# Two f32 transformer blocks on one core: token halves in a fixed order where token-major layers end, three held pieces of weights, the FFN input in wide operations, an even rate for the modulation

## The chip, the cores and the metric

The kernel runs on one core of one Trainium2 chip. The metric is device time of one launch in microseconds (us). All arithmetic that counts is f32: a matmul operand is split into a rounded high part and a low remainder, and three matmuls (high·high, high·low, low·high) stand for one product.

## The reference

Two blocks over 256 tokens and width 2048. The part that the change touches is the end of the first block, its FFN, and every layer whose result is wanted with tokens on partitions:

```python
mod = (c @ w_mod[l] + b_mod[l]).reshape(B, N_MOD, D)          # six segments of 2048
shift_f, scale_f, gate_f = mod[:, 3, None], mod[:, 4, None], mod[:, 5, None]
...
mix_out = merged @ w_out[l]
x = x + gate_m * rms_norm(mix_out, g_post_mix[l])
h2 = rms_norm(x, g_pre_ffn[l]) * (1 + scale_f) + shift_f
f = (jax.nn.silu(h2 @ w_ffn_gate[l]) * (h2 @ w_ffn_up[l])) @ w_ffn_down[l]
x = x + gate_f * rms_norm(f, g_post_ffn[l])
...
x = x + (y * jax.nn.silu(gate)) @ w_out_a[i]                   # second block, first layer
x = x + (merged * jax.nn.silu(gate)) @ w_out_b[i]              # second block, last layer
return rmsnorm(x, norm_f)
```

## The kernel before

Weights come from HBM in loads of 1 MB (`raw`, three buffers, issued on SP's queue). `stream_` cuts each load into pieces of 1024 columns: ACT casts a piece to its high part `wh` (L134), DVE subtracts to get `wl` (L135). There are three buffers of each (`SPL`), so a fourth piece can be cast only when TensorE is done with the first.

Most layers (`lin`) give features on partitions. Token-major layers (`linT`: w_out, the FFN's gate and up weights w_fgu, w_ffn_down as w_fd, w_outa, w_outb) give 128 tokens on partitions: there are two token halves, h = 0 and 1, each with its own PSUM banks, and every piece is used for both (12 matmuls of 512 columns in a piece, six in each half). A piece is used at once for both halves, except that the last load's two pieces are held and used for half 0 first, then for half 1.

The order of instructions on each engine is not the written one. A list scheduler with its own model of times takes whatever it holds ready, the written order being the priority; so it may interleave the halves. `issue_after(i)` pins what a block writes behind instruction i on its engine. `high_priority` lets weight loads and splits go ahead of older work; from the first block's second part on (`first`), all pieces have it.

`post` is the end of w_out and of w_fd: for each half, square sums from PSUM (ACT, L252), times a gate row (DVE, L930), the row statistic (DVE, then a power on GpSimd, L260), the update of x in four slices (DVE, L922), its square sums (ACT). Behind w_out the FFN input follows: the statistic again, x scaled into `mix` (ACT, L725), TensorE transposes 128x128 blocks into PSUM (L729, L739), and `modulated` makes each chunk of 128 features: high part on ACT (L714), scaled value on DVE (L715), low part on DVE (L716). Chunks 0 to 7 are made half by half, chunks 8 to 15 for both halves. Then the FFN starts; `XF` (Fh, Fl) is its input. Behind w_fd x is transposed (`turned`, L241) and split to `A`, the input of w_ina.

The matrix-vector product c @ w_mod is made by the side, one tile of 128x1024 (0.5 MB) at a time (`mod_tile`: a load on SP's queue and one DVE operation, L460). 96 tiles belong to the first block; `side` asks for `rate` of them at every 1 MB weight load. `mod_flush` sums 16 tiles over partitions on TensorE (L442). The last 32 of the 96 are the shift of the FFN input. In w_fd, `H(k)` splits two chunks of the hidden state at a time (L339 on ACT, L340 on DVE) into one of four places of `hx`, and keeps the last pair for the calls that follow.

Of the kernel before, what the change touches and what calls it, by code (L numbers as in the profile page):

```python
# [9 lines left out]
F32 = mybir.dt.float32  # L10
F32R = mybir.dt.float32r
AF = mybir.ActivationFunctionType
ALU = mybir.AluOpType
# [3 lines left out]
P = 128  # L17
T = 256
D = 2048
KC = D // P  # L20
# [6 lines left out]
SPL = 3  # L27
# [1 line left out]
SCALE = 128.0 ** -0.5  # L29


ORDER = "m2 m3 m4 G2 g9 g10 k0 k1 v7 v8 S r3 Q A r4 p0 p1 p2 G3 p3"

PACE = (3, 1)

# [54 lines left out]
class Kern:  # L90
# [19 lines left out]
    def stream(self, src, n, per):  # L110
        return list(self.pieces(src, n, per))

    def pieces(self, src, n, per):

        got = self.stream_(src, n, per)
        for a in range(0, n, per):
            if self.first:
                with self.tc.high_priority():
                    hl = next(got)
                if self.side and a + per >= n:  # L120
                    self.side()
            else:
                hl = next(got)
            yield hl

    def stream_(self, src, n, per):

        nc = self.nc
        raw = self.wp.tile([P, 2048], F32, name="raw", tag="raw", bufs=RAW)
        self.load = nc.sync.dma_start(raw[:, :n], src)  # L130
        for a in range(0, n, per):
            wh = self.wp.tile([P, 1024], F32R, name="wh", tag="wh", bufs=SPL)
            wl = self.wp.tile([P, 1024], F32R, name="wl", tag="wl", bufs=SPL)
# [63 lines left out]
    def linT(self, W, sb, X, nk, kper, ncols, which="a", lead=0, mid=None):  # L197
# [5 lines left out]
        ng = nk // kper  # L203
        mm = self.nc.tensor.matmul

        def run(h, k, wh, wl, o):
            xh, xl = X(k)
            t = slice(h * P, (h + 1) * P)
            for q in range(nq):
                w = slice(o + q * 512, o + q * 512 + 512)  # L210
                mm(banks[h][q], xh[:, t], wh[:, w], start=k == 0, stop=False, skip_group_check=True)  # L211
                mm(banks[h][q], xh[:, t], wl[:, w], start=False, stop=False, skip_group_check=True)  # L212
                mm(banks[h][q], xl[:, t], wh[:, w], start=False, stop=k == nk - 1, skip_group_check=True)  # L213
# [11 lines left out]
        for kg in range(ng):  # L225
            for i, (wh, wl) in enumerate(self.pieces(W[sb, kg], kper * ncols, 1024)):
                held.append((kg * kper + i * pk, wh, wl))
# [243 lines left out]
    def block1(self, c1):  # L471
        nc, tc, A = self.nc, self.tc, self.A
# [216 lines left out]
            self.row_in(0, grow[i], i * 1024, 1024)  # L689
        gs = self.cp.tile([P, 16], F32, name="gsf")  # L690

        def between(s, last):
            if s == 0:
                with tc.issue_after(last.ins):
                    self.load_x(nc.scalar)
            if s == 2:
                self.side = None
                for t in todo:
                    self.mod_tile(new, *t)
                self.mod_flush()  # L700
                nc.vector.scalar_tensor_tensor(gs, self.mods[:, 64:80], 1.0, self.vcol("g_pre_ffn", 0, 16), ALU.add, ALU.mult)

        mix = [p1e.tile([P, 8 * T], F32, name="mix%d" % h, tag="E1", bufs=2) for h in range(2)]
        ss, update = self.post(A["w_out"], XO, KC, mix, lambda c: grow[c // 2][:, c % 2 * 512:c % 2 * 512 + 512],
                               between=between)
# [12 lines left out]
        xn = []  # L718
        for h in range(2):
            update(h)  # L720
            self.rsum(r, ss, h)
            for c in range(4):

                m = mix[h][:, c * 512:(c + 1) * 512]
                nc.scalar.activation(m, self.xt[h][:, c * 512:(c + 1) * 512], AF.Copy, scale=r[:, h:h + 1])  # L725
                if c < 2:
                    bank = self.acc("b")
                    for b in range(4):
                        nc.tensor.transpose(bank[:, b * P:(b + 1) * P], m[:, b * P:(b + 1) * P], self.ident)  # L729
                    tmp = self.sp.tile([P, 512], F32, name="tm", tag="th", bufs=2)  # L730
                    for b in range(4):
                        s = slice(b * P, (b + 1) * P)
                        modulated(4 * c + b, slice(h * P, (h + 1) * P), bank[:, s], tmp[:, s])
        for k in range(8, KC, 2):
            bank = self.acc("b")
            tmp = self.sp.tile([P, 512], F32, name="tm", tag="th", bufs=2)
            for b in range(2):
                for h in range(2):
                    nc.tensor.transpose(bank[:, b * T + h * P:b * T + (h + 1) * P], mix[h][:, (k + b) * P:(k + b + 1) * P],  # L739
                                        self.ident)  # L740
                s = slice(b * T, (b + 1) * T)
                modulated(k + b, slice(0, T), bank[:, s], tmp[:, s])

# [156 lines left out]
    def post(self, W, X, nk, mix, G, wide=False, between=None):  # L900

        nc = self.nc
        nq = 2 if wide else 1
        last = 4 // nq - 1
        sm, sx = self.sums("sm4"), self.sums("sx4")
        r = self.rtile()
        for s in range(last + 1):
            banks = self.linT(W, s, X, nk, 2 if wide else 4, nq * 512, which="ba"[s % 2] if wide else "a")
            if s == last:
                break  # L910
            for h in range(2):
# [12 lines left out]
        return sx, update  # L924
# [175 lines left out]
    def ffn(self):  # L1100
        nc, tc, A = self.nc, self.tc, self.A
        with ExitStack() as c:
# [28 lines left out]

            for s in range(FFN // 256):

                banks = self.linT(A["w_fgu"], s, self.XF, KC, 4, 512, lead=0 if s else 3, mid=mid)
                t = self.sp.tile([P, 512], F32, name="ht", tag="sw", bufs=3)
                g = self.sp.tile([P, 512], F32, name="gt", tag="gt", bufs=2)
                for h in range(2):
                    a, bank = slice(h * T, (h + 1) * T), banks[h][0]
                    self.silu2(g[:, a], bank[:, :T], T)
                    nc.vector.tensor_mul(t[:, a], g[:, a], bank[:, T:])  # L1140
                due.append((s, t))
                for _ in range(3):
                    if todo and s:
                        with tc.issue_after(ready.ins):
                            self.mod_tile(new, *todo.pop(0))
                if s == 14:
                    self.mod_flush()
# [161 lines left out]
    def add_out(self, W, X, row=None, each=None, final=None):  # L1309
# [163 lines left out]
```

## Time and profile before

| | us |
|---|---|
| median of 3 runs (2441.3 to 2444.39) | 2444.15 |
| the profiled execution | 2438.1 |
| its span, first to last instruction | 2436.1 |
| TensorE busy in it | 2378.1 (98%) |
| VectorE (DVE) busy | 1678.5 (69%) |
| ScalarE (ACT) busy | 1246.7 (51%) |
| GpSimd (POOL) busy | 19.3 (1%) |
| mean granted TensorE clock | 0.991 |

The profiled execution is 6.05 us below the median of the runs. Times in the profile are from the start of the span. PE is TensorE, PEld its weight loads, SP the queue that issues DMAs. A matmul's duration includes its way through the array; matmuls overlap, so the distance from start to start counts, not the duration.

### The profile page before, as it was taken

Reading aid. Unit: us, or ns where it says so; the run is one execution under the profiler, and the core shown is the slowest. Engines: PE = TensorE matmul, PEld = TensorE weight load, DVE = VectorE, ACT = ScalarE, POOL = GpSimd, SP = SyncE. Lnnn points to the kernel's source line nnn. Section 1 sums busy time; section 2 is a strip of 40 time slices with the busy share of each in tenths; the row PEclk is TensorE's granted clock in tenths of the full one; section 3 lists DMA queues with packets and bytes.
Section 4 is the critical chain, followed back from the end, with each engine's and each line's share of the span. In section 5 each row is a group of like instructions: output and inputs, shape, how many; then the busy total and the mean of one; then the engine's idle time right before and its main releaser. Section 6 shows DMA issues by size and latency. Waiting matters only on the chain.

```text
span 2436.1 us, 37172 instructions
## 1 busy us (share of the span) xinstructions
PE 2378.1 (98%) x15142; PEld 2153.9 (88%) x15142; DVE 1678.5 (69%) x2213; ACT 1246.7 (51%) x1716; POOL 19.3 (1%) x30
## 2 busy tenths in 40 slices
PE   7999999999989999999999989999999999999997
PEld 6899989999868888888888879998898899999986
DVE  8997898888777575555556566756664477777764
ACT  5877674534464444444445454445644455554543
POOL 0000000000000000000000000000000000000000
PEclk9999999999999999999999999999999999999999
DMA  9997557999948585555555545555655544454453
GB/s 365 349 365 259 182 177 272 329 350 333 350 161 321 191 291 193 190 189 187 194 197 200 190 149 191 191 189 186 228 193 190 190 163 167 158 189 169 161 190 138
DMA packets 104043, 540.61 MB, mean 222 GB/s; under 512 B 9888, under 2 KB 18240, under 8 KB 53184
## 3 DMA queue, kind: packets, MB, share of 16 engines
q1 hardware_dynamic: 100896, 526.19, 60.8%
q10 hardware_dynamic: 2160, 8.88, 1.0%
q0 software_dynamic: 816, 3.16, 0.4%
q8 instruction: 118, 1.93, 0.3%
q14 instruction: 53, 0.43, 0.1%
HBM read 533.99 MB, written 4.21 MB: 221 GB/s over the span
## 4 chain that ended last, share of the span: by engine, by line
PE 94%; DVE 2%; ACT 1%; DMA 1%; issue 1%; POOL 0%; SPq 0%; DVEq 0%; POOLq 0%
PE acca L145 15%; PE acca L144 15%; PE acca L146 15%; PE acca L212 11%; PE acca L211 11%; PE acca L213 11%; PE acca L193 2%; PE acca L194 2%; PE acca L192 2%; PE accb L212 2%; PE accb L213 2%; PE accb L211 2%; DMA hid<-in_w_mod_dram 1%; DVE wl L135 1%; PE accb L1343 1%
## 5 line engine op out<-in xcount | busy, mean ns | idle before, releaser
L135 DVE TENSOR_TENSOR wl<-raw,wh 128x1024 fp32r<-128x1024 f32 x802 | 977.9, 1221 | 570.9 <-ACT wh L134 568.3
L134 ACT CAST wh<-raw 128x1024 fp32r<-128x1024 f32 x802 | 841.7, 1051 | 864.0 <-PE acca L213 377.9
L145 PE MATMUL acca<-Ql,wh 128*128 128x256 f32 x1024 | 290.5, 284 | 0.0
L144 PE MATMUL acca<-Qh,wh 128*128 128x256 f32 x1024 | 289.8, 284 | 0.0
L146 PE MATMUL acca<-Qh,wl 128*128 128x256 f32 x1024 | 285.5, 281 | 0.0
L212 PE MATMUL acca<-wl,Fh 128*128 128x512 f32 x704 | 276.8, 393 | 1.0 <-DVE wl L135 0.9
L213 PE MATMUL acca<-wh,Fl 128*128 128x512 f32 x704 | 275.7, 393 | 0.3 <-DVE Fl L716 0.3
L211 PE MATMUL acca<-wh,Fh 128*128 128x512 f32 x704 | 252.3, 396 | 1.7 <-ACT Fh L714 1.7
L144 PE MATMUL acca<-xh,wh 128*128 128x256 f32 x832 | 232.8, 284 | 4.5 <-ACT xh L808 3.4
L145 PE MATMUL acca<-xl,wh 128*128 128x256 f32 x832 | 233.7, 284 | 0.0
L146 PE MATMUL acca<-xh,wl 128*128 128x256 f32 x832 | 227.0, 283 | 0.0
L144 PEld LDWEIGHTS acca<-Qh,wh 128*128 128x128 f32 x1024 | 192.9, 188 | 0.5
L145 PEld LDWEIGHTS acca<-Ql,wh 128*128 128x128 f32 x1024 | 192.6, 188 | 0.8
L146 PEld LDWEIGHTS acca<-Qh,wl 128*128 128x128 f32 x1024 | 192.1, 189 | 0.4
L144 PEld LDWEIGHTS acca<-xh,wh 128*128 128x128 f32 x832 | 158.1, 190 | 7.3 <-ACT xh L808 3.6
L145 PEld LDWEIGHTS acca<-xl,wh 128*128 128x128 f32 x832 | 157.4, 189 | 1.6 <-issue 0.7
L212 PEld LDWEIGHTS acca<-wl,Fh 128*128 128x128 f32 x704 | 132.7, 189 | 29.1 <-DVE wl L135 2.2
L211 PEld LDWEIGHTS acca<-wh,Fh 128*128 128x128 f32 x704 | 131.3, 188 | 30.0 <-ACT Fh L714 2.9
L213 PEld LDWEIGHTS acca<-wh,Fl 128*128 128x128 f32 x704 | 132.4, 188 | 28.6 <-DVE Fl L716 1.5
L146 PEld LDWEIGHTS acca<-xh,wl 128*128 128x128 f32 x832 | 155.1, 190 | 1.3 <-issue 1.0
L145 PE MATMUL acca<-Al,wh 128*128 128x256 f32 x512 | 143.7, 282 | 0.0
L144 PE MATMUL acca<-Ah,wh 128*128 128x256 f32 x512 | 142.7, 281 | 0.0
(374 smaller groups left out, 4600.5 us busy)
## 6 DMA issues: line engine op xcount, KB each, us to landing
raw<-in_w_fgu_dram SPq DMA_DIRECT2D x88, 1024.0 KB, 4.8
raw<-in_w_inb_dram SPq DMA_DIRECT2D x64, 1024.0 KB, 4.8
raw<-in_w_in_dram SPq DMA_DIRECT2D x51, 1024.0 KB, 6.3
rawm<-in_w_mod_dram SPq DMA_DIRECT2D x96, 512.0 KB, 5.7
raw<-in_w_fd_dram SPq DMA_DIRECT2D x44, 1024.0 KB, 4.8
raw<-in_w_ina_dram SPq DMA_DIRECT2D x32, 1024.0 KB, 4.8
raws<-in_w_mod_dram SPq DMA_DIRECT2D x30, 1024.0 KB, 8.4
raw<-in_w_in_g_dram SPq DMA_DIRECT2D x16, 1024.0 KB, 7.2
```

What stands on the lines that cost most here:

```text
L134: nc.scalar.copy(wh[:, :per], raw[:, a:a + per])
L135: nc.vector.tensor_sub(wl[:, :per], raw[:, a:a + per], wh[:, :per].bitcast(F32))
L144: mm(out, ah, bh, start=start, stop=False, skip_group_check=True)
L145: mm(out, ah, bl, start=False, stop=False, skip_group_check=True)
L146: mm(out, al, bh, start=False, stop=stop, skip_group_check=True)
L192: mm(banks[h], xh[:, t], wh[:, s], start=fresh and k == 0, stop=False, skip_group_check=True)
L193: mm(banks[h], xh[:, t], wl[:, s], start=False, stop=False, skip_group_check=True)
L194: mm(banks[h], xl[:, t], wh[:, s], start=False, stop=k == nk - 1, skip_group_check=True)
L211: mm(banks[h][q], xh[:, t], wh[:, w], start=k == 0, stop=False, skip_group_check=True)
L212: mm(banks[h][q], xh[:, t], wl[:, w], start=False, stop=False, skip_group_check=True)
L213: mm(banks[h][q], xl[:, t], wh[:, w], start=False, stop=k == nk - 1, skip_group_check=True)
L1343: nc.tensor.matmul(ps[:, g * T:(g + 1) * T], q[g][:, P:T], kT, start=g == 0, stop=g == 1, skip_group_check=True)
```

## The change

Seven edits. (1) `linT` holds the last `hold` pieces (2, or 3 in the last column block of w_out, w_fd, w_outa and w_outb) and pins half 1's matmuls behind half 0's last one. (2) `H` drops its places when called with k = 0 and keeps two pairs, since three held pieces span two pairs. (3) The first two pieces of the FFN's weights are split ahead of w_out's last column block, into four buffers that the modulation used (rawm0, rawm1, mac, qll), each 128x1024. (4) The FFN's first `linT` is called right behind the input's chunks 0 to 7, with three pieces at first and the transposes of chunks 8 to 15 (`rest`) after them; its other pieces are no longer ahead of older work. (5) Chunks 4 to 15 are made by `wide`, four (or two) chunks in one go over 512 elements: DVE multiplies out of PSUM, GpSimd adds the shift, ACT casts, DVE subtracts. (6) The upper half of x is scaled into `mix` by GpSimd, not ACT. (7) The rate of modulation tiles is 2.2 per load throughout; it was 3, then 4 from the attention on.

```diff
-ORDER = "m2 m3 m4 G2 g9 g10 k0 k1 v7 v8 S r3 Q A r4 p0 p1 p2 G3 p3"
+ORDER = "m2 m3 m4 G2 g9 g10 k0 k1 v7 v8 S r2.2 Q A p0 p1 p2 G3 p3"
...
-            if self.first:
+            if self.first and high:
...
+            if new:
+                wh, wl = (f() for f in new.pop(0))
+            else:
+                wh = self.wp.tile([P, 1024], F32R, name="wh", tag="wh", bufs=SPL)
...
         def flush():
+            last = None
             for h in range(2):
-                for k, wh, wl in held:
-                    for c in range(pk):
-                        run(h, k + c, wh, wl, c * ncols)
+                with ExitStack() as c:
+                    if h and len(held) > 1:
+                        c.enter_context(self.tc.issue_after(last.ins))
+                    for k, wh, wl in held:
+                        for i in range(pk):
+                            last = run(h, k + i, wh, wl, i * ncols)
             held.clear()
...
-                if n >= lead and kg < ng - 1:
+                if lead <= n <= total - hold:
                     flush()
-            if kg == 0 and mid:
-                mid()
+                if mid and n == max(lead, 2):
+                    mid()
...
+                new = [[lambda t=t: p1.tile([P, 1024], F32R, name="w" + t, tag=t, bufs=1) for t in two]
+                       for two in (("rawm0", "rawm1"), ("mac", "qll"))]
+                early.extend(self.pieces(A["w_fgu"][0, 0], 2048, 1024, new))
...
+        def wide(k, n, t, bank):
+
+            bc = lambda g: g[:, :, None].to_broadcast([P, n, 512 // n])
+            tmp = self.sp.tile([P, 512], F32, name="tm", tag="th", bufs=2).rearrange("p (n t) -> p n t", n=n)
+            hl = [x.tiles[k // 8][:, k % 8:k % 8 + n, t] for x in (fh, fl)]
+            nc.vector.tensor_mul(tmp, bank.rearrange("p (n t) -> p n t", n=n), bc(gs[:, k:k + n]))
+            nc.gpsimd.tensor_tensor(tmp, tmp, bc(self.mods[:, 48 + k:48 + k + n]), ALU.add)
+            self.ready = self.split(*hl, tmp)
+
...
+                if c < 2:
+                    nc.scalar.activation(m, x, AF.Copy, scale=r[:, h:h + 1])
+                else:
+                    nc.gpsimd.tensor_scalar(m, x, r[:, h:h + 1], None, ALU.mult)
...
+        self.first_banks = self.linT(A["w_fgu"], 0, self.XF, KC, 4, 512, lead=3, early=early, mid=rest)
...
-            banks = self.linT(W, s, X, nk, 2 if wide else 4, nq * 512, which="ba"[s % 2] if wide else "a")
+            banks = self.linT(W, s, X, nk, 2 if wide else 4, nq * 512, which="ba"[s % 2] if wide else "a",
+                              hold=3 if s == last else 2)
...
             def H(k):
+                if k == 0:
+                    got.clear()
                 i = k // 2
-                if got.get("i") != i:
+                if i not in got:
...
-                    got.update(i=i, hl=(h, l))
-                h, l = got["hl"]
+                    got.pop(i - 2, None)
+                    got[i] = h, l
+                h, l = got[i]
...
-            banks = self.linT(W, s, X, KC, 4, 512)
+            banks = self.linT(W, s, X, KC, 4, 512, hold=3 if s == 3 else 2)
```

## Rows read from the trace of the kernel before

**Rows 1.** Stretches: busy us (xcount) of PE, PEld, DVE, ACT, POOL; clock; DMA share; GB/s.

```profile
426.00:661.00 235.00, 235.00 (x1737) 223.81 (x1737) 197.81 (x207) 108.97 (x149) 1.76 (x3) 1.00 0.93 341
687.00:703.00 16.00, 8.23 (x27) 5.72 (x28) 12.52 (x31) 14.58 (x37) 1.63 (x3) 0.68 0.19 67
703.00:720.00 17.00, 16.73 (x79) 13.10 (x78) 16.43 (x39) 11.71 (x21) 0.00 (x0) 1.00 0.38 128
1190.00:1436.00 246.00, 246.00 (x1089) 203.63 (x1088) 141.91 (x139) 119.24 (x142) 1.07 (x2) 1.00 0.57 198
```

**Rows 2.** Timeline where w_out ends: start, us, engine, line, operation, idle before.

```profile
684.56 0.60 ACT L252 ACTIVATE sqt<-acca 128x512 f32<-128x512 f32 x1 [2.35 <-PE acca L213]
...
686.18 0.39 PE L213 MATMUL acca<-wh,xo 128*128 128x512 f32 x1
...
686.31 0.57 POOL L260 TENSOR_TENSOR rt<-mst,mhalf 128x1 f32<-128x1 f32 x1 [63.98 <-DVE mst L259]
...
686.33 1.24 DVE L135 TENSOR_TENSOR wl<-raw,wh 128x1024 fp32r<-128x1024 f32 x1
...
687.49 2.72 DVE L922 SCALAR_TENSOR_TENSOR x<-mix,rt,x 128x512 f32<-128x512 f32 x4
...
693.05 1.97 PE L729 MATMUL accb<-cst,mix 128*128 128x128 f32 x8 [6.49 <-ACT mix L725]
...
695.85 0.79 PE L211 MATMUL acca<-wh,Fh 128*128 128x512 f32 x1 [0.83 <-ACT Fh L714]
```

**Rows 3.** Groups by line, 680 to 725 us: busy us, mean ns of one.

```profile
L714 ACT ACTIVATE Fh<-accb,mods,gsf 128x128 fp32r<-128x128 f32 (+1 forms) x24 | 10.6, 490 | 4.7 <-PE accb L739 4.4 <-DVE tm L715 0.2
L715 DVE TENSOR_SCALAR tm<-accb,gsf,mods 128x128 f32<-128x128 f32 (+1 forms) x24 | 10.2, 450 | 3.2 <-ACT Fh L714 2.9
L716 DVE TENSOR_TENSOR Fl<-tm,Fh 128x128 fp32r<-128x128 f32 (+1 forms) x24 | 7.2, 328 | 0.2
```

**Rows 4.** Timeline where w_fd ends and w_ina begins.

```profile
1437.23 0.60 ACT L252 ACTIVATE sqt<-acca 128x512 f32<-128x512 f32 x1 [0.30 <-PE acca L213]
...
1438.16 0.39 PE L213 MATMUL acca<-wh,hx 128*128 128x512 f32 x1
...
1439.72 1.59 POOL L260 TENSOR_TENSOR rt<-mst,mhalf 128x1 f32<-128x1 f32 x1 [116.18 <-DVE mst L259]
...
1441.35 2.74 DVE L922 SCALAR_TENSOR_TENSOR x<-f,rt,x 128x512 f32<-128x512 f32 x4 [0.46 <-POOL rt L260]
...
1444.81 0.58 ACT L252 ACTIVATE sqt<-acca 128x512 f32<-128x512 f32 x1
...
1453.22 0.39 PE L144 MATMUL acca<-Ah,wh 128*128 128x256 f32 x1
```

**Rows 5.** Operations on hx, 1190 to 1436 us: min/median/max ns.

```profile
L339 ACT ACTIVATE hx<-hid x40: 632/632/637, 1203.9 to 1416.6; 128x512 fp32r<-128x512 f32 x40
L340 DVE SCALAR_TENSOR_TENSOR hx<-hid,hx x40: 678/694/694, 1204.6 to 1417.3; 128x512 fp32r<-128x512 f32 x40
```

**Rows 6.** Timeline where w_outb, the last layer, ends.

```profile
2416.78 1.22 DVE L135 TENSOR_TENSOR wl<-raw,wh 128x1024 fp32r<-128x1024 f32 x1 [1.50 <-ACT wh L134]
...
2422.72 0.69 DVE L1317 TENSOR_TENSOR x<-x,acca 128x512 f32<-128x512 f32 x1 [4.71 <-PE acca L213]
...
2423.85 0.69 DVE L1317 TENSOR_TENSOR x<-x,acca 128x512 f32<-128x512 f32 x1 [0.45 <-PE acca L213]
...
2426.23 1.12 POOL L260 TENSOR_TENSOR rt<-mst,mhalf 128x1 f32<-128x1 f32 x2 [666.86 <-DVE mst L258]
```

**Rows 7.** Timeline of GpSimd and DVE about 291 us.

```profile
290.91 3.21 POOL L981 TENSOR_TENSOR rsd<-mv,mhalf 128x2 f32<-128x2 f32 x1 [21.25 <-DVE mv L979]
...
291.22 2.34 DVE L135 TENSOR_TENSOR wl<-raw,wh 128x1024 fp32r<-128x1024 f32 x2
```

**Rows 8.** Modulation tiles: DVE, 360 to 673 us; last sums on TensorE.

```profile
L460 DVE SCALAR_TENSOR_TENSOR mac<-rawm,vec,mac x77: 1261/1278/1286, 367.4 to 668.1; 128x1024 f32<-128x1024 f32 x77
...
676.86 1.84 PE L442 MATMUL accb<-cst,rawm 128*128 128x1 f32 x16
```

More of the change, by code (lines that the diff above doesn't have):

```diff
@@ L111, in stream, with pieces, stream_ @@
         return list(self.pieces(src, n, per))
-    def pieces(self, src, n, per):
-        got = self.stream_(src, n, per)
+    def pieces(self, src, n, per, new=None, high=True):
+        got = self.stream_(src, n, per, new)
         for a in range(0, n, per):
-            if self.first:
+            if self.first and high:
                 with self.tc.high_priority():
                     hl = next(got)
-                if self.side and a + per >= n:
-                    self.side()
             else:
                 hl = next(got)
+            if self.side and a + per >= n:
+                self.side()
             yield hl
-    def stream_(self, src, n, per):
+    def stream_(self, src, n, per, new=None):
         nc = self.nc
@@ L131, in stream_ @@
         for a in range(0, n, per):
[L132 to L133 removed]
+            if new:
+                wh, wl = (f() for f in new.pop(0))
+            else:
+                wh = self.wp.tile([P, 1024], F32R, name="wh", tag="wh", bufs=SPL)
+                wl = self.wp.tile([P, 1024], F32R, name="wl", tag="wl", bufs=SPL)
             nc.scalar.copy(wh[:, :per], raw[:, a:a + per])
@@ L195, in linA, with linT @@
         return banks
-    def linT(self, W, sb, X, nk, kper, ncols, which="a", lead=0, mid=None):
+    def linT(self, W, sb, X, nk, kper, ncols, which="a", hold=2, lead=0, early=(), mid=None):
         nq = ncols // 512
@@ L202, in linT @@
         pk = 1024 // ncols
-        ng = nk // kper
+        total = nk // pk
         mm = self.nc.tensor.matmul
@@ L212, in run @@
                 mm(banks[h][q], xh[:, t], wl[:, w], start=False, stop=False, skip_group_check=True)
-                mm(banks[h][q], xl[:, t], wh[:, w], start=False, stop=k == nk - 1, skip_group_check=True)
+                last = mm(banks[h][q], xl[:, t], wh[:, w], start=False, stop=k == nk - 1, skip_group_check=True)
+            return last
         held = []
         def flush():
+            last = None
             for h in range(2):
-                for k, wh, wl in held:
-                    for c in range(pk):
-                        run(h, k + c, wh, wl, c * ncols)
+                with ExitStack() as c:
[4 more added lines that the diff above has]
+                            last = run(h, k + i, wh, wl, i * ncols)
             held.clear()
         n = 0
-        for kg in range(ng):
-            for i, (wh, wl) in enumerate(self.pieces(W[sb, kg], kper * ncols, 1024)):
-                held.append((kg * kper + i * pk, wh, wl))
+        for kg in range(nk // kper):
+            if kg == 0 and early:
+                got = early
+            else:
+                got = self.pieces(W[sb, kg], kper * ncols, 1024, high=not early)
+            for wh, wl in got:
+                held.append((n * pk, wh, wl))
                 n += 1
-                if n >= lead and kg < ng - 1:
+                if lead <= n <= total - hold:
                     flush()
-            if kg == 0 and mid:
-                mid()
+                if mid and n == max(lead, 2):
+                    mid()
         flush()
@@ L690, in block1 @@
         gs = self.cp.tile([P, 16], F32, name="gsf")
+        rawm = new
         def between(s, last):
@@ L698, in between @@
                 for t in todo:
-                    self.mod_tile(new, *t)
+                    self.mod_tile(rawm, *t)
                 self.mod_flush()
                 nc.vector.scalar_tensor_tensor(gs, self.mods[:, 64:80], 1.0, self.vcol("g_pre_ffn", 0, 16), ALU.add, ALU.mult)
+                new = [[lambda t=t: p1.tile([P, 1024], F32R, name="w" + t, tag=t, bufs=1) for t in two]
+                       for two in (("rawm0", "rawm1"), ("mac", "qll"))]
+                early.extend(self.pieces(A["w_fgu"][0, 0], 2048, 1024, new))
+        early = []
         mix = [p1e.tile([P, 8 * T], F32, name="mix%d" % h, tag="E1", bufs=2) for h in range(2)]
@@ L722, in block1 @@
             for c in range(4):
-                m = mix[h][:, c * 512:(c + 1) * 512]
-                nc.scalar.activation(m, self.xt[h][:, c * 512:(c + 1) * 512], AF.Copy, scale=r[:, h:h + 1])
+                x, m = (t[:, c * 512:(c + 1) * 512] for t in (self.xt[h], mix[h]))
+                if c < 2:
+                    nc.scalar.activation(m, x, AF.Copy, scale=r[:, h:h + 1])
+                else:
+                    nc.gpsimd.tensor_scalar(m, x, r[:, h:h + 1], None, ALU.mult)
                 if c < 2:
@@ L729, in block1, with rest @@
                         nc.tensor.transpose(bank[:, b * P:(b + 1) * P], m[:, b * P:(b + 1) * P], self.ident)
[L730 to L742, printed above, removed]
+                    t = slice(h * P, (h + 1) * P)
+                    if c:
+                        wide(4, 4, t, bank)
+                    else:
+                        tmp = self.sp.tile([P, 512], F32, name="tm", tag="th", bufs=2)
+                        for b in range(4):
+                            s = slice(b * P, (b + 1) * P)
+                            modulated(b, t, bank[:, s], tmp[:, s])
+        def rest():
+            for k in range(8, KC, 2):
+                bank = self.acc("b")
+                for b in range(2):
+                    for h in range(2):
+                        nc.tensor.transpose(bank[:, b * T + h * P:b * T + (h + 1) * P],
+                                            mix[h][:, (k + b) * P:(k + b + 1) * P], self.ident)
+                wide(k, 2, slice(0, T), bank)
+        self.first_banks = self.linT(A["w_fgu"], 0, self.XF, KC, 4, 512, lead=3, early=early, mid=rest)
     def evict(self, banks, dst):
@@ L1132, in ffn @@
             for s in range(FFN // 256):
-                banks = self.linT(A["w_fgu"], s, self.XF, KC, 4, 512, lead=0 if s else 3, mid=mid)
+                banks = self.linT(A["w_fgu"], s, self.XF, KC, 4, 512, mid=mid) if s else self.first_banks
                 t = self.sp.tile([P, 512], F32, name="ht", tag="sw", bufs=3)
```

1 line of the change is left out of this document (removed).

## The prediction, written before the run

> **What bounds the kernel now.** I read the busy line first: TensorE is busy 98% of the span, so only what TensorE waits for can be won, and what lies before its first and behind its last matmul. Then I went through its idle gaps in the timeline. In the long stretches it never waits: in w_fd it starts 1089 matmuls in 246.00 us, 0.226 us apart at full clock [rows 1], and from 426 to 661 us, where the modulation is loaded beside the weights, it has no gap either. What is left stands in three places that the change touches.
>
> The first is the end of w_out and the FFN input. The last matmul of w_out ends at 686.57 us, TensorE then idles 6.49 us until the first transpose, and its first FFN matmul waits again [rows 2]. From 687 to 720 us it starts 27 + 79 matmuls, of which 32 are transposes of 128 columns; 74 at 0.226 and 32 at half of that are 20.3 us of work in 33. With the 0.43 us before, 13.1 us are lost here. The clock stood at 0.68 in the first half of it (part of the time at 1.2 instead of 2.4 GHz, after the idle time), ACT was busy 14.58 of 16 us, and in the second half DVE was busy 16.43 of 17 [rows 1]: once it has begun, the making of F sets the pace. The second place is the end of w_fd: last matmul done at 1438.55, first of w_ina at 1453.22, 14.7 us that hold only 32 transposes [rows 4]. The third is the end: from about 2423.82, where half 1 is done [rows 6], to the span's end at 2436.1, 12.3 us.
>
> In all three a half's chain (square sums, power, update) can start only when that half is done. ACT's first square shows when: 2.0 us before the end in w_out, 1.35 us in w_fd, and by DVE's addition 1.13 us in w_outb [rows 2, 4, 6]. So today the halves end almost together.
>
> **The change, part by part.** Held pieces and order: with three pieces held and half 1 pinned behind half 0, half 0 is done 18 matmuls, 18 x 0.226 = 4.07 us, before the end. This moves no work; it costs something only if the third held piece is not split in time. In w_outb its wl ends at 2418.00 [rows 6] and would be wanted 24 matmuls before the end, at 2418.39: 0.4 us to spare. One DVE operation of 0.69 to 1.28 us in front of it would cost TensorE 0.3 to 0.9 us at a place; I take 0. Where two pieces are held the second is wanted at the same moment as now or later, and TensorE does not wait there now: 0.
>
> FFN input, start: half 0's chain begins 4.07 - 2.0 = 2.05 us earlier. Its power was ready at 686.88, but DVE's update began at 687.49, since a weight split lay in between [rows 2]; the two early pieces are split ahead of this, which saves another 0.6. Together 2.7; at least 2.0.
>
> FFN input, supply: of L715 and L716's 17.4 us on DVE [rows 3], 8 of 24 calls stay, 8 x 0.778 = 6.2. Six `wide` calls come, each a multiplication out of PSUM and a subtraction of 512 elements, 0.69 each by L1317 and L340 [rows 5, 6]: 8.3. That saves 2.9, and a split of 1.24 us for each early piece leaves this stretch: 5.4 of the 28.95 us that DVE was busy here. ACT saves as much on L714 (10.6 to 3.9 + 6 x 0.632 = 7.7) and four scalings besides. How much of DVE's 5.4 us reaches TensorE is bounded by 0 (the clock, or GpSimd's new part, sets the pace) and 5.4 (DVE alone does). I take half, 2.8, as DVE is the bound in one half of the stretch. Sum for this place: -5.5 us, from -2.0 to -8.1.
>
> GpSimd's new part: six additions and four scalings of 512 elements. No row shows such an operation. Below, DVE's 0.69 us for the same elements; above, the 3.21 us of its longest operation [rows 7]. I take 0.69 plus its own shortest operation, 0.57 [rows 2]: 1.26, so 12.6 us in all, hidden behind 30 us of TensorE's work as long as DVE lets it run. In GPSIMD Engine Reference, section 3.1, the Trainium skill gives about 2.6 cycles per element for a two-input operation; at its 1.2 GHz an estimate from it is 1.1 us for 512 elements and 11 us for ten, which no run here shows yet, and the sum would be the same.
>
> End of w_fd: the first bank of half 0 was done 1.35 us before the end; it will be done 21 matmuls, 4.75 us, before it: 3.4 us earlier. The power, the update, half 1's square (1444.81, behind half 0's on ACT) and the transposes hang on it one after the other [rows 4]. Against it: w_ina's first three pieces come free 2.7, 1.4 and 0 us before the end, go ahead of older work, and take DVE 1.2 us each; now none lies inside the update (1441.35 to 1444.09), and then one or two will. I take off 1.6: -1.8 us, from 0 to -3.4.
>
> A cost that is easily missed: `H`. `linT` calls X(k) once for each half. In w_fd's first piece k = 0 is called for half 0 and again for half 1, and each call with k = 0 clears `got`. So the pair is split twice, once too many in each of w_fd's two blocks, into the place that half 0's matmuls still read. The second split can't start before these have read it, and all that follows needs the pair or stands behind in the same banks: nothing covers it. ACT 0.63 and DVE 0.69 [rows 5], less two matmuls (0.45) that need the high part alone, are 0.9 us; behind a weight cast and split in both queues (1.05 and 1.22) up to 3.1. I take 1.2 each: +2.4 us, from +1.8 to +6.2.
>
> The end: half 0's outputs leave almost wholly under half 1's matmuls. From half 1's addition at 2423.85 to its power's end at 2427.35 are 3.5 us, with half 0's two multiplications, statistics and power in between [rows 6]; alone I count 2.5. From there to the end, 8.75 us hold eight output DMAs of 256 KB; four go earlier, and at the 341 GB/s of [rows 1] four take 3.1 us. Of this I take 2.4, as the last DMA's own latency stays. Sum -3.4 us, from -0.5 to -4.1.
>
> Rate: a load is 24 matmuls, 5.4 us, so 2.2 tiles for each is one in 2.5 us. Served are 77 main operations in 301 us [rows 8], one in 3.9, with the DMA engines 0.93 busy [rows 1]. What is asked stays above what is served, so the pace stays that of the DMAs: 0. The last sums end at 678.70, 7.9 us before w_out ends.
>
> Sum: -5.5 - 1.8 + 2.4 - 3.4 = -8.3 us on the profiled execution, 2438.1 to 2429.8. That execution is 6.05 us below the median of the runs; I keep the difference: 2444.15 - 8.3 = 2435.9, so 2436.
>
> **The rivals.** GpSimd and DVE in turns: the power issued at 290.91 us on two elements took 3.21 us, and ended 0.56 us after two weight splits of DVE, back to back, were over [rows 7]; the one beside a split at the end of w_fd took 1.59 [rows 4], against 0.57 otherwise. So GpSimd stands still while DVE reads two tensors. If its 12.6 us and DVE's remaining 23.6 can't overlap, they are 36 us in a stretch of 33: the supply saves nothing, and waiting powers eat most of the start. The place gives 0.5 instead of 5.5: -3.3 in all, 2441. On this the Trainium skill has a rule (SBUF — State Buffer, section "Who interferes with whom"): a DVE operation with two SBUF inputs and a GpSimd operation that reads SBUF exclude each other for a whole instruction. By that rule the trace's 3.21 us is explained, and the change's additions would also hold up DVE.
>
> The order buys nothing: the third held piece is late at every place (spare 0.4 us), TensorE waits what half 0 gains. Then 2.0 of the first, the 1.8 and about 2 of the end are gone: -2.5, 2442. For it speaks how small the spare time is, against it that DVE has nothing else then in w_fd and w_outb.
>
> More than forecast: the shorter idle time keeps the clock up and both chains move whole: 8.1 + 3.4 + 4.1 - 1.8 = 13.8, 2430. The clock fell in both places before, and the idle time is still some 3.8 us in the first, so less likely.
>
> Slower: the modulation is late. With a lower rate its tiles lose priority against the attention's work where DVE is 198 of 235 us busy [rows 1], and the DMAs can't make it up. The shift is its last segment, and the early pieces need its buffers. It has 7.9 us until w_out ends and some 5 more until the first F: from 13 us late on each microsecond costs one, from 21 late on (six tiles of 3.9 less) the kernel is slower than before. At 30 it is 2453.
>
> **How the numbers follow.** A measurement of this kernel tells apart about 0.2%, 4.9 us. Forecast (5 to 11 us faster) 0.50, more 0.15, turns 0.19, order for nothing 0.09, late modulation 0.07. The likeliest gives 2436, its own range 2433 to 2439. Up to 2444 the range takes in turns and order, down to 2428 most of "more", which leaves under 0.2 outside. Faster by over 0.2%: 0.50 + 0.15 and 0.05 from the upper rivals' better half, 0.70; slower 0.07; the rest, 0.23, within.
>
> **What would show it.** ACT's first square about 4 us before the last matmul of w_out and w_fd, and the first transposes within 4 us after w_out; L339 and L340 with 46 instead of 44 splits (two more) and two TensorE gaps of about 1 us at k = 0 of w_fd; the span ending about 9 us after the last matmul. GpSimd operations of over 2 us in the FFN input mean the turns. Wrong would be a last L442 behind w_out's end, or new TensorE gaps between 360 and 680 us, where I expect none.

## The result and the profile after

The changed kernel takes 2461.68 us (2461.26 to 2462.14, four runs) against 2442.91 us before, a ratio of 1.0079 with an interval of 1.0066 to 1.0092: 18.8 us slower. The profiled execution takes 2461.26 us, its span 2459.4 us; that is 23.3 us longer than the span before, 4.5 us more than the medians say, as the profiled execution of the kernel before was a quick one (2438.1 us). The forecast was 2436 us. Times below are from the start of a span; what TensorE *loses* in a stretch is what the distances from one matmul's start to the next exceed the usual one of its form, summed up.

Stretches of the changed kernel (us, busy us (xcount) of PE, PEld, DVE, ACT, POOL; clock; DMA share; GB/s):

```profile
403.00:434.00 31.00, 31.00 (x264) 30.60 (x262) 16.91 (x27) 18.60 (x41) 0.00 (x0) 1.00 0.52 185
...
426.00:638.00 212.00, 212.00 (x1626) 204.41 (x1625) 175.89 (x184) 96.86 (x131) 0.00 (x0) 1.00 0.88 331
638.00:674.00 36.00, 17.93 (x67) 14.32 (x66) 24.35 (x23) 5.41 (x8) 1.77 (x3) 0.72 0.77 274
674.00:708.00 34.00, 34.00 (x159) 28.44 (x158) 23.24 (x26) 15.59 (x20) 0.57 (x1) 1.00 0.75 281
```

From 426 to 638 us TensorE never waits, as in [rows 1]. Then 18 of 36 us are gone, at a place that the prediction named as free of gaps. w_out's last matmul ends at 708.85 us instead of 686.57 [rows 2]: 22.3 of the span's 23.3 us. The timeline there:

```profile
642.21 1.28 DVE L473 SCALAR_TENSOR_TENSOR rawm<-rawm,vec,mac 128x1024 f32<-128x1024 f32 x1
643.54 0.80 PE L455 MATMUL accb<-cst,rawm 128*128 128x1 f32 x3 [4.91 <-DVE rawm L473]
...
646.98 0.37 PE L282 MATMUL accb<-cst,Gm 128*16 128x128 f32 x1
647.39 0.26 ACT L284 COPY gT<-accb 16x128 f32<-16x128 f32 x1 [7.09 <-PE accb L282]
647.96 0.67 POOL L285 DMA_DIRECT2D grow<-gT  x1 [356.52 <-ACT gT L284]
651.30 1.22 POOL L288 DMA_DIRECT2D gr<-grow  x2 [2.67 <-DMA grow<-gT]
657.79 1.29 DVE L969 TENSOR_TENSOR mix<-acca,gr 128x512 f32<-128x512 f32 x2 [3.22 <-DMA gr<-grow]
658.63 0.77 PE L215 MATMUL acca<-wh,xh 128*128 128x512 f32 x1 [11.28 <-DVE mix L969]
671.85 0.50 PE L216 MATMUL acca<-wl,xh 128*128 128x512 f32 x1 [1.89 <-DVE wl L138]
```

Read it from below. At 658.63 TensorE had idled 11.28 us for DVE's L969, which takes w_out's banks away times the gate row `gr`; by the code the four banks were then full. The row came late: transposed at 646.98, copied, written to HBM, read back, landed about 657.8. The transposition stands on TensorE directly behind the fifth of six sums of the modulation (L455), and for that sums TensorE had idled 4.91 us already, since its last tile was done by DVE only at 643.5. The row did not need these sums: the gate is the first segment, complete with the second sums, and DVE had made its factor `Gm` at 482.3. Only the order of TensorE's instructions put the transposition behind the fifth:

```profile
L696 DVE TENSOR_TENSOR Gm<-mods,vec x1: 176/176/176, 482.3 to 482.3; 128x16 f32<-128x16 f32 x1
```

In the kernel before, the sixth and last sums starts at 676.86 [rows 8] and the fifth at 612.4: the fifth is 31 us late. The waits are 18.1 us; the granted clock stood at 0.50 from 643.5 to 658.6 and at 0.51 to 664 us, which made the sums 1.7 and the 13 matmuls behind 2.4 us longer. Together 22.2. The stretches (columns as above):

```profile
643.50:647.30 3.80, 3.75 (x17) 3.50 (x17) 0.90 (x3) 0.00 (x0) 0.00 (x0) 0.50 0.86 305
647.30:658.60 11.30, 0.05 (x1) 0.00 (x1) 5.88 (x7) 0.26 (x1) 1.77 (x3) 0.50 0.75 266
658.60:664.00 5.40, 5.37 (x13) 4.24 (x14) 5.33 (x6) 0.00 (x0) 0.00 (x0) 0.51 0.56 205
```

Why 31 us late? The first sums, in the changed kernel and (second fence) in the one before:

```profile
432.55 0.27 PE L1093 MATMUL accb<-cst,e 128*128 128x128 f32 x1
432.66 0.50 PE L455 MATMUL accb<-cst,rawm 128*128 128x1 f32 x4
433.03 0.41 PE L1093 MATMUL accb<-cst,e 128*128 128x128 f32 x2
433.28 1.40 PE L455 MATMUL accb<-cst,rawm 128*128 128x1 f32 x12
```

```profile
400.54 0.27 PE L1054 MATMUL accb<-cst,e 128*128 128x128 f32 x1
400.65 0.50 PE L442 MATMUL accb<-cst,rawm 128*128 128x1 f32 x4
```

Both stand right behind a head's `e` in the attention: the sixth head's now, the second's before. The last tile of these sums was ready in time (DVE, 395.93 to 397.21), but its buffer stays taken until TensorE has summed it. Tiles take three buffers in turn, so the third load after it needs the same buffer, and all later loads of tiles stand behind that one on SP's queue:

```profile
402.29 0.33 SPq L466 DMA_DIRECT2D rawm<-in_w_mod_dram  x1
409.12 0.33 SPq L130 DMA_DIRECT2D raw<-in_w_in_dram  x1
415.03 7.62 SPq L130 DMA_DIRECT2D raw<-in_w_pa_dram  x2
429.61 0.33 SPq L130 DMA_DIRECT2D raw<-in_w_in_g_dram  x1
434.71 4.96 SPq L466 DMA_DIRECT2D rawm<-in_w_mod_dram  x2
```

For 32 us no tile is loaded; the DMA engines are 0.52 busy from 403 to 434 us and DVE 16.9 of 31 us, where the kernel before has 0.82 and 27.0:

```profile
403.00:434.00 31.00, 31.00 (x261) 30.70 (x261) 27.02 (x34) 16.56 (x33) 0.00 (x0) 1.00 0.82 300
```

From there on the DMA engines are 0.88 busy and nothing is made up. The place follows from the code. `mod_flush`, which writes the sums, is called when the 18th tile is asked for. At 3, 3, 4, 4, 4 tiles that is at the fifth load after `S`, at 2.2 at the ninth (19.8). From the third load on each writes one head: two heads stand in front before, six now. In the trace heads are 7.25 us apart here; four are 29 us, measured 32.

### The profile page after: what moved, and what is told of

Its sections match the earlier page's. It is cut to its first block, busy times and chain, and to the rows that moved or that the text cites. A ratio compares the mean times of both kernels' runs of the same rounds, so it can differ in the third digit from the quotient of the medians.

```text
span 2459.4 us, 37181 instructions
## 1 busy us (share of the span) xinstructions
PE 2384.6 (97%) x15142; PEld 2158.9 (88%) x15142; DVE 1680.5 (68%) x2195; ACT 1242.0 (51%) x1704; POOL 30.3 (1%) x40
## 4 chain that ended last, share of the span: by engine, by line
PE 90%; DVE 4%; DMA 3%; ACT 1%; issue 1%; POOL 0%; SPq 0%; POOLq 0%; DVEq 0%; ACTq 0%
PE acca L148 15%; PE acca L147 15%; PE acca L149 15%; PE acca L216 10%; PE acca L217 10%; PE acca L215 10%; DMA hid<-in_w_mod_dram 2%; PE acca L196 2%; PE acca L197 2%; PE acca L195 2%; PE accb L215 2%; PE accb L216 2%; PE accb L217 2%; DVE wl L138 1%; DVE hid L473 1%
```

## The experiments

All run beside the kernel before (medians 2441.9 to 2443.0 us in their groups). This fence gathers from their traces when the sums start on TensorE, what TensorE idled for the gate row (the wait for the fifth sums and the one for `gr`), and when w_out ends:

```
run            first   second  fifth   idled for the row  w_out ends  median us
before         400.7   446.2   612.4   0                  686.6       2442.9
e2             432.5   477.4   643.4   4.9 + 12.4         711.7     2462.0
e1_rate34      402.4   447.9   613.9   0                  692.7       2442.0
e13            405.6   451.9   618.0   0                  695.1       2448.6
e11_rate3      410.6   465.9   635.2   6.6                704.2       2455.8
e9             362.8   470.7   635.1   5.6                702.9       2454.9
e10            430.3   478.5   644.7   4.7 + 12.6         709.2       2460.5
changed        432.7   477.5   643.5   4.9 + 11.3         708.9       2461.7
e3_row_early   432.2   477.1   656.8   0                  685.7       2447.0
```

**The rate of before, all else changed.**

```diff
-ORDER = "... S r2.2 Q A p0 p1 p2 G3 p3"
+ORDER = "... S r3 Q A r4 p0 p1 p2 G3 p3"
```

> The change with the rate of before (3, then 4 tiles per load). Theory 'rate': the 18.6 us that TensorE waits at 643, 658 and 672 us go, and the rest of the change nets to about nothing: 2442 us (2438 to 2446), last square of w_out's half 0 near 683 us. Rival 'order': the waits come from the held pieces, the pinned halves and the two early pieces, which all stay: 2455 us or more, with the gaps still there.

Measured 2441.99 us, 1.0000 (0.9991 to 1.0008) of before. The three gaps are gone: the rate made all of the loss, and in the medians the rest nets to nothing. Smaller gaps stay at 666 us; they are taken up below.

**The rate alone, in the kernel before.** The reverse edit in the other kernel.

> The kernel before with the rate 2.2 alone. Theory 'rate': slower by the same waits in w_out, 2443 + 19 = 2462 us (2458 to 2466), some 13 tiles issued behind w_out's twelfth load. Rival 'order': 2443 us, no gap between 600 and 680 us.

Measured 2461.95 us, 1.0079 (1.0065 to 1.0093): the changed kernel's own figure. 15 tiles are issued behind w_out's twelfth load (6 at the rate of before), about as many as expected. But they are not left over: by the code all 96 are asked for by w_out's sixth load, and they come late.

**The gate row earlier.** `Gm` and `row_out(0, Gm)` are moved ahead of the third column block of w_in_g2.

> The change at rate 2.2, with the transposition and the way out of the gate row written two column blocks earlier, ahead of the fifth sums. Theory 'leftover tiles': the 11.65 us gap at 658 goes, but w_out's thirteenth load still stands behind 13 tiles on SP's queue and lands no earlier than about 675 us, so TensorE waits for weights instead: 4 to 8 us are won, 2454 to 2458 us. Rival 'gate row': its place behind the fifth sums is the whole cost, 2443 to 2446 us.

Measured 2446.95 us, 1.0019 (1.0010 to 1.0028). 14.7 of 18.7 us come back: the row's place was most of the cost, as the rival said, though its 2446 us is missed by 1. w_out's thirteenth load is issued at 649.9 instead of 675.3 us, so the tiles did not hold up the weights. But the sums are later still (the fifth by another 13 us; why is not shown), and w_out's end now meets the next one that waits, the shift:

```profile
704.36 0.80 PE L455 MATMUL accb<-cst,rawm 128*128 128x1 f32 x3 [18.66 <-DVE rawm L473]
```

This is the late modulation that the prediction described, at the place it described, and it costs 5 us against e1_rate34.

**H without the second split.** The rate of before, and in `H`:

```diff
-                if k == 0:
+                if k == 0 and 0 not in got:
                     got.clear()
```

> The rate of before, and H keeps the first pair when it is called for the second half (no second split at k = 0). Theory 'second split costs': 2.5 us faster than the run with the rate alone, 2439.5 us, two TensorE gaps at the two starts of w_fd's column blocks gone. Rival 'covered': within 0.5 us of that run.

Measured 2441.66 us, 0.9995 (0.9986 to 1.0003), 0.3 us below e1_rate34. That is in the rival's range, but the two intervals don't shut out 2.5 us either. The traces decide: in w_fd TensorE loses 2.3 us in e1_rate34 (0.7 at the first block's start, 1.8 at the second's) and -0.2 here, so the second splits cost 2.5. Both gaps are gone, and L352 and L353 split hx 44 instead of 46 times.

**Without the early pieces** (the two `early` lines in `between` deleted).

> From here on everything at the rate of before and with no second split in H (2441.7 us). This one without the two early pieces: the FFN's first load stands behind w_out's last one again. Theory 'buffer': the early load lands about 20 us before the last modulation tile frees its places and holds one of three raw buffers so long, which made the 2.10 and 0.92 us gaps at 666 us and the lost 4.4 us there; without it 2438 us (2437 to 2439.5). Rival 'cover': the first pieces' splits then fall into the FFN input, 2442 us or more.

Measured 2440.19 us, 0.9991 (0.9982 to 1.0000), between the two forecasts: the ratio falls by 0.0004, 1 us, less than the noise. The traces show more. In w_out's last 110 us TensorE loses 4.3 us in every run at the old rate with early pieces and -0.2 in every one without. The early load is issued at 648.21 in e1_rate34; its two pieces are cast when the last tiles free their places, and until then it holds one of three raw buffers, so w_out's next casts, and TensorE behind them (second fence), come late:

```profile
665.30 1.98 ACT L137 CAST wh<-raw 128x1024 fp32r<-128x1024 f32 x2
668.83 1.04 ACT L137 CAST wrawm<-raw 128x1024 fp32r<-128x1024 f32 x1 [1.54 <-DVE mac L473]
...
675.82 1.04 ACT L137 CAST wmac<-raw 128x1024 fp32r<-128x1024 f32 x1
```

```profile
666.39 0.50 PE L215 MATMUL acca<-wh,xh 128*128 128x512 f32 x1 [1.71 <-ACT wh L137]
```

**Only held pieces and order** (as the last, and the FFN input and its first `linT` as before).

> Only the held pieces and the fixed order of the halves are left of the change: neither early pieces nor wide operations, the FFN input as before. Theory 'order pays, input does not': the ends of w_fd and of the kernel win 2.5 and 2.7 us against before, half 0's earlier start about 1 us more: 2437 us (2435.5 to 2439). Rival 'input pays too': 2441 us or more, as the wide operations' part of the gain is missing.

Measured 2439.84 us, 0.9992 (0.9983 to 1.0001), again between the forecasts. The ends win 2.2 us (w_fd) and 3.1 us (the kernel's end), as expected; at w_outa 1.1 us are lost, where the third held piece is split too late; in the FFN input 14.4 us are lost instead of 13.4.

**Without wide operations** (`wide` calls `modulated` chunk by chunk, ACT scales all of x; with early pieces).

> With the early pieces, but each chunk made by itself and all of x scaled by ACT, as before. Theory 'latency': the input's 7 us without matmuls are a chain of one half, not DVE's or ACT's load, so wide operations are worth under 1 us: 2441 to 2443 us. Rival 'supply' (the prediction's 2.8 us): 2444.5 us or more.

Measured 2440.95 us, 0.9994 (0.9985 to 1.0003), no slower than with them. In the FFN input (the 40 us from w_out's end) TensorE loses 13.0 us here and 12.8 in e4_rate34_h; 14.4 in e6_order_only and 13.2 in e5_no_early. By these pairs wide operations are worth 0.2 to 1.1 us. That is no more than one and the same input differs by: e1_rate34 loses 11.1 us there and e4_rate34_h 12.8, at a granted clock of 0.87 and 0.50 between 8 and 16 us behind w_out's end.

**The next splits pinned.**

```diff
+            if pin and kg in (1, 2):
+                with ExitStack() as c:
+                    for i in pin:
+                        c.enter_context(self.tc.issue_after(i.ins))
+                    got = list(got)
```

> The next weights' casts and splits (loads 2 and 3 of the FFN) pinned behind half 0's statistic on DVE and behind its second scaling on ACT. Theory 'in the way': one cast (1.02 us) among the squares and one split (1.24 us) ahead of the statistic took the start's gain; 2.3 us less idle before the first transposition (4.4 instead of 6.7 us): 2439.4 us. Rival 'late weights': TensorE then waits for the third piece, 2441.5 us or more.

`pin` holds half 0's statistic on DVE and its second scaling on ACT. Measured 2443.96 us, 1.0004 (0.9995 to 1.0013), in the rival's range. The start came as expected and was given back, not by the third piece but by F:

```profile
696.02 0.69 PE L770 MATMUL accb<-cst,mix 128*128 128x128 f32 x2 [3.69 <-ACT mix L762]
...
699.82 0.79 PE L215 MATMUL acca<-wrawm,Fh 128*128 128x512 f32 x1 [1.83 <-ACT Fh L740]
...
705.65 0.80 PE L217 MATMUL acca<-wrawm,Fl 128*128 128x512 f32 x1 [4.61 <-DVE Fl L742]
```

3.7 us of idle time instead of 6.7, then 1.8 and 4.6, since the splits now stand ahead of half 1's update and of Fl. The input loses 14.1 us in all, against 12.8. So an earlier start alone does not pay; that DVE's and ACT's load is then the limit fits this, but was not tested by itself.

**First sums early, and late.** Two schedules of the whole change, and a third with rate 3:

```diff
-ORDER = "... S r2.2 Q A p0 p1 p2 G3 p3"
+ORDER = "... S r9 Q r0 A p0 p1 p2 r2.2 G3 p3"           # e9
+ORDER = "... S r3 Q r1.8 A p0 p1 p2 r8 G3 r4 p3"        # e10
+ORDER = "... S r3 Q A p0 p1 p2 G3 p3"                   # e11
```

> The whole change; of the rate only the first 18 tiles are asked for sooner (9 for each of the two loads ahead of the attention, none for the six loads in it, then 2.2 again), so that the first sums are written ahead of the eight heads, and every later sums at the same load as in the change. Theory 'first sums' (written behind six heads instead of two, they hold a tile's buffer for four heads of 7.25 us, and all later tiles are that much later): first sums at about 400 us, no stretch without tiles, no gaps in w_out: 2442 us (2440 to 2446). Rival 'asked too late' (a tile comes no earlier than the rate asks for it, all along): the later sums stay some 20 to 30 us late, 2455 us or more.

> The whole change; rate 3, then 1.8 for the six loads in the attention, then 8 for four loads, then 4: the first sums are written at the same load as in the change, behind six heads, but the second sums already two loads later, and from there on more tiles are asked for than in the kernel before. Theory 'first sums': first sums at 432 us, the rest some 30 us late, as slow as the change, 2458 to 2463 us. Rival 'asked too late': caught up by the higher rate, 2442 to 2447 us.

> The whole change with rate 3 throughout: the first sums are written behind three heads, one more than at the rate of before. Theory 'first sums': all sums some 7 to 11 us later than at the rate of before (first at about 411, last near 686 to 690 us), the gate row still in time, so at most 2 us slower than that run: 2442 to 2444 us. Rival 'proportional' (cost grows with each head: 18.7 us for four): 4.7 us, 2446.5 us or more.

Measured 2454.90 us, 1.0053 (1.0040 to 1.0065); 2460.54 us, 1.0080 (1.0066 to 1.0094); 2455.83 us, 1.0054 (1.0042 to 1.0067). The late one fell out as 'first sums' said: more tiles asked for than before, and nothing caught up. Its sums and the wait for the row:

```profile
430.14 0.27 PE L1093 MATMUL accb<-cst,e 128*128 128x128 f32 x1
430.25 0.28 PE L455 MATMUL accb<-cst,rawm 128*128 128x1 f32 x2
...
644.71 0.37 PE L455 MATMUL accb<-cst,rawm 128*128 128x1 f32 x1 [4.68 <-DVE rawm L473]
...
661.07 0.77 PE L215 MATMUL acca<-wh,xh 128*128 128x512 f32 x1 [12.55 <-DVE mix L969]
```

In the other two that theory was too narrow. The rival was right about e9, and e11 is 13.9 us slower than before, far more than either forecast priced. In e9 the *second* sums stand behind the last head, and hold up the tiles again:

```profile
470.58 0.27 PE L1093 MATMUL accb<-cst,e 128*128 128x128 f32 x1
470.69 0.28 PE L455 MATMUL accb<-cst,rawm 128*128 128x1 f32 x2
```

At 470.7 they are 24.5 us late, and the fifth 22.7; with rate 3 the second is 19.7 late, the fifth 22.8. So each sums has its place on TensorE, the tiles run ahead of it by three buffers only, and in these runs a delay is carried on to within 3 us. The price is not in proportion: 1.5 us late cost nothing, 22.7 and 22.8 cost 5.6 and 6.6 us of idle time, 31.1 and 32.3 cost 16.2 and 17.3. By these two groups some 15 to 17 us are free, an estimate, and each microsecond beyond costs about one.

**Rate 4 through the attention, 2.2 behind it.**

```diff
+ORDER = "... S r4 Q A p0 p1 p2 G3 r2.2 p3"
```

> The whole change; rate 4 up to the eighth head's loads, 2.2 from there to the end of w_out. The first two sums are written at the same loads as at the rate of before, the later ones at 1, 4 and 7 loads later. Theory 'written place, then the DMAs' (a sums never comes before the load at which it is written; from there on the tiles go at the DMAs' pace, so a delay is neither made up nor made larger): first two sums at about 401 and 447 us, fifth at 612 to 616, 2442 us (2440 to 2445). Rival 'the low rate itself' (a lower priority of the tiles while w_in_g, w_pb and w_out are loaded): fifth sums 10 us late or more and 2447 us or more.

Measured 2448.55 us, 1.0024 (1.0014 to 1.0034). The time is in the rival's range, but its sign did not come: the fifth sums are 5.6 us late, not 10, and the first are already 4.9 late, so the low rate behind the attention adds 0.7, and TensorE does not wait for the row. Part of the time goes before the attention begins: between 240 and 260 us TensorE loses 9.2 us, in e9 9.4, 2.9 to 7.2 in the eleven runs with rate 3 there, and only 2.3 in the three with 2.2. 12 tiles are issued by 360 us (18 in e9) instead of 10 or 8, and DVE's work on them stands among the first splits there. That is 2 to 6 of the 6.6 us above e1_rate34; the rest stays open.

**What paid, and the change repaired.** The first is e6_order_only with two pieces held at w_outa. The second is the whole change with the rate of before, no second split, no early pieces, and two pieces at w_outa:

```diff
+            banks = self.linT(W, s, X, KC, 4, 512, hold=3 if s == 3 and row is not None else 2)
```

> What paid, alone: the run with only the held pieces and the fixed order, and two pieces instead of three at w_outa, where the third came 1.1 us late. Theory: w_fd's end 2.2, the end of the kernel 3.1 us better than before, nothing lost: 1.1 us below the run with three pieces there, 2438.5 us (2437 to 2440.5). Rival: no better than before, 2442 us.

> The change repaired: the rate of before, no second split in H, no early pieces, two pieces held at w_outa; held pieces elsewhere, fixed order and wide input stay. By the gaps of the runs so far: w_fd's end -2.2, the end of the kernel -3, w_outa 0, input 0 to -1 against before: 2438 us (2436 to 2440). Rival: the wide input costs what it saves, same as the run without it, 2440 us.

Measured 2440.35 us, 0.9992 (0.9983 to 1.0001), and 2437.76 us, 0.9981 (0.9972 to 0.9989). At w_outa nothing is lost in either. The first is not clear of noise. The repaired change is faster than both kernels, by 4.3 us than the one before; its trace wins 2.5 us at w_fd's end and 2.8 at the kernel's end, and 0.1 in the FFN input. Yet its profiled span, 2438.0 us, is not below that of before, 2436.1: it loses 3.1 us more between 240 and 260 us and 3.5 more behind the input, in work that the two share. The wide input is all that tells the two runs apart: 2.6 us by the medians, 0.4 by the traces of the input (13.6 and 13.2). Its worth stays open between these.

## Why the prediction was wrong

**Rate: 0.** This step failed. It set one tile in 2.5 us asked for against one in 3.9 us served, both as means: the first with w_out's 5.4 us for a load, where a load of the attention takes 7.25; the second over 301 us [rows 8], though from 402.7 to 434 us the kernel before issues 11 tiles, one in 2.8. Above all it took tiles for a flow. The sums are instructions of TensorE with a place of their own, and the prediction did not ask what is queued behind them: a tile's buffer, and behind this SP's loads of tiles. In place of 0 the rate cost some 19 us: e1_rate34 and e2 show that it was the rate, e10 that the place of the sums does it and not the number of tiles asked for, e3_row_early that most of the price is the gate row's. Of the signs of being wrong that the prediction named, new gaps between 360 and 680 us came.

**The slow rival** had the mechanism, late modulation, at 0.07, and the wrong place: it priced the shift behind w_out, the last segment, and not the gate, the first, whose row is wanted in the middle of w_out. e3_row_early shows that its own place would have been next, and tests its terms: the last sums are 27.5 us late there and the input loses 9.5 us more than in the changed kernel (22.4 against 12.8), so some 18 us were free, not 13. The 15 to 17 us that are free at the row belong to another wait; that they lie near the forecast 13 is luck.

**FFN input, start: -2.7.** The earlier squares came, the gain did not. The first square stands 4.04 us ahead of w_out's last matmul's end, as forecast, but the transpositions come no sooner:

```profile
704.80 0.60 ACT L265 ACTIVATE sqt<-acca 128x512 f32<-128x512 f32 x1 [3.02 <-PE acca L217]
...
707.16 2.74 DVE L961 SCALAR_TENSOR_TENSOR x<-mix,rt,x 128x512 f32<-128x512 f32 x4 [0.69 <-POOL rt L273]
...
709.72 1.03 ACT L137 CAST wh<-raw 128x1024 fp32r<-128x1024 f32 x1
709.81 3.49 DVE L138 TENSOR_TENSOR wl<-raw,wh 128x1024 fp32r<-128x1024 f32 x3
...
711.80 0.19 ACT L265 ACTIVATION_READ_ACCUMULATOR sqt<-x 128x1 f32 x1
...
713.22 0.15 DVE L271 TENSOR_REDUCE mst<-sx 128x1 f32<-128x4 f32 x1
...
715.54 1.97 PE L760 MATMUL accb<-cst,mix 128*128 128x128 f32 x8 [6.69 <-ACT mix L754]
```

A cast stands among the squares (1.03), and three splits of the pieces that come next hold DVE until 713.30, 1.3 us after the squares are done. The prediction saw that the old split left this place, not that others take it; e8_pin, which moves them, has 3.0 us less idle time there.

**FFN input, supply: -2.8.** 0.2 to 1.1 us by the pairs of e4 to e7. It took half of DVE's saving as TensorE's, a guess between two bounds. By the timeline GpSimd's additions stand in each wide chunk's chain (1.04 us each), and its scalings slow DVE (below); what each of these costs TensorE is not shown. The early pieces were counted as a gain of 0.6 and cost 4.3 in w_out at the rate of before. So the place gave -0.6 in this pair (13.4 lost before, 12.8 after) instead of -5.5; over all traces the old input loses 13.4 to 14.4 us (four runs) and the changed one 11.1 to 13.1 (seven), 1.7 less in the mean.

**GpSimd.** Ten operations took 13.6 us; forecast 12.6. This fence holds the two groups of the changed kernel (busy us, mean ns of one):

```profile
L756 POOL TENSOR_SCALAR mix<-x,rt 128x512 f32<-128x512 f32 x4 | 7.1, 1791 | 0.1
L744 POOL TENSOR_TENSOR tm<-tm,mods 128x512 f32<-128x512 f32 x6 | 6.5, 1091 | 5.8 <-DVE tm L743 5.8
```

The turns of the rival did not come: one operation of ten took over 2 us.

**w_fd's end: -1.8, H: +2.4, tail: -3.4.** Right, within their bounds: -2.5 (lost 11.4 before, 8.9 after), +2.5, and -2.7 (12.25 us from the last matmul's end to the span's end before, 9.51 after).

```profile
1225.34 0.50 PE L215 MATMUL accb<-wh,hx 128*128 128x512 f32 x1 [0.47 <-ACT hx L352]
...
1347.25 0.50 PE L215 MATMUL acca<-wh,hx 128*128 128x512 f32 x1 [1.57 <-ACT hx L352]
...
1461.36 0.60 ACT L265 ACTIVATE sqt<-acca 128x512 f32<-128x512 f32 x1 [2.57 <-PE acca L217]
...
1768.16 0.50 PE L216 MATMUL acca<-wl,Yh 128*128 128x512 f32 x1 [0.82 <-DVE wl L138]
```

The first two are the second splits at k = 0; the idle times stand in brackets, with the slower starts around them they are the 2.5 us. The first square of w_fd's end stands 4.5 us ahead of the last matmul's end, 1.32 before [rows 4]. **Held pieces: 0** held for w_outb, which the prediction worked out, and not for w_outa, which it took along: 1768.16 is its third piece, 1.1 us in all.

The terms as measured: 22.3 - 0.6 + 2.5 - 2.5 + 1.1 - 2.7 = 20.1 of the span's 23.3 us. Another 3.1 are lost between the input and w_fd; that stretch loses 2.7 to 8.6 us from run to run (8.4 in e12_best, which has the old input), and no part of the change could be tied to it.

## What to carry to other kernels

Work by the side is not a flow: find the instruction on a busy engine that closes each portion of it, ask what stands in front of that instruction in the written order and which buffer it holds meanwhile. Where a rate is changed, lay the cumulative count over the written work, load by load, instead of comparing means. When a chain is started sooner, look at what becomes ready in the place that it leaves; and ask of a buffer that is filled early how long it is held.

## What was not expected of the hardware

DVE's update L961 takes 0.75 us a slice (2.74 for four at 707.16). Beside GpSimd's scaling four took 3.61, and slices that meet the start of one 1.19 and 1.17; without GpSimd (e6_order_only) all are 0.75:

```profile
715.25 3.31 POOL L756 TENSOR_SCALAR mix<-x,rt 128x512 f32<-128x512 f32 x2
...
715.28 3.61 DVE L961 SCALAR_TENSOR_TENSOR x<-mix,rt,x 128x512 f32<-128x512 f32 x4 [1.06 <-POOL rt L273]
```

On this the Trainium skill (SBUF — State Buffer, section "SBUF: two separate sides") says that of such a pair the one that starts first gets the shared ports for its whole instruction and the other blocks. The trace agrees in kind only: DVE lost 0.45 us at each start, not a whole scaling of 1.57, and the slice from 716.39 to 717.13 took 0.74 while scalings ran.

On GpSimd a scaling by a column, with one tensor read, took 1.57 to 2.20 us, longer than an addition of two tensors of the same 512 elements, 1.04 to 1.35. All four scalings met DVE operations that read two tensors, so their time alone is not shown. For the addition the figure of the Trainium skill (GPSIMD Engine Reference, section 3.1) gave an estimate of 1.1 us, and the trace agrees.
